# A two-layer hybrid encoder on one core: a static list scheduler gets other durations, a port rule and a table of priorities per layer

## The chip, the cores and the metric

The kernel runs on one core of a Trainium2 chip. The core has a matrix engine (PE, whose weight loads are listed apart as PEld), three engines for elementwise work (VectorE, listed as DVE; ScalarE, ACT; GpSimd, POOL) and SyncE (SP), whose queue issues nearly all transfers of this kernel. The metric is the device time of one execution, in microseconds (us).

## The reference

Two layers with `D_MODEL` 1024, 1024 tokens and a feed-forward width of 2816, all in float32. Each layer projects the residual stream once and gives the columns to four mixers: a Conformer convolution (31 taps), a bidirectional complex state-space layer (S5, 16 groups of 16 channels, 64 states each), a short gated convolution, and a differential attention with four heads. Cut to the loop over the layers:

```python
for l in range(DEPTH):
    h = jnp.einsum('bsd,de->bse', x, w_in[l])
    y_a = conformer_conv(h[..., :OFF_S5], ...)
    y_b = s5_mixer(h[..., OFF_S5:OFF_SC], ...)
    y_c = short_gated_conv(h[..., OFF_SC:OFF_DA], sc_conv_w[l])
    ...                       # q, k, v from h, partial rotary embedding of q and k
    y_d = diff_attention(q, k, v, lam, da_subln_g[l], lam_init)
    mix = jnp.einsum('bse,ed->bsd', jnp.concatenate([y_a, y_b, y_c, y_d], axis=-1), w_out[l])
    x = layer_norm(DEEPNORM_ALPHA * x + mix, ln1_g[l], ln1_b[l])
    ff = jax.nn.silu(x @ w_ffn1[l]) * (x @ w_ffn3[l])
    x = layer_norm(DEEPNORM_ALPHA * x + ff @ w_ffn2[l], ln2_g[l], ln2_b[l])
```

## The kernel before

**Arithmetic.** Matrix products keep float32 accuracy by splitting each operand into a high and a low part: a cast makes the high part, a subtraction the low one, and each product is three matmuls (`mm3`, L491; `split`, L497). So weights cost elementwise work: a cast and a `tensor_tensor` for each piece of 128x512. The products with the first and third feed-forward weights go by Winograd's form of Strassen's scheme: seven products in place of eight, and more additions on the weights (`make_unit`, L1335) and on the tokens (`token_operands`, L1283).

**Stages of a layer.** First the input blocks (`mixers_in`, L1430): per block of 256 columns either `chan_gemm` (psum tile `cg`) or `tok_gemm` (psum tile `tg`), and beside them the S5 layer in eight pairs of groups. A pair has tables (`s5_pair_tables`, L818; tiles `s5t`, made from the parameter tile `P`), then chunk sums, two scans and outputs (`s5_pair`, L876; work tiles `s5k`, psum tiles `s5wp`, `s5v`, `s5y`). The long convolution (`conf_conv`, L993) is a chain of multiply-adds into `acc` on DVE, then PE transposes (`cvt` there, `cvb` back) for its LayerNorm. Then come keys, values and queries (`kst`, `stg`, `vq` tiles), eight query tiles of attention (`sc` scores, `probs`, transposes `atp` to `aT`, `po` outputs), the output projection (`wo`) with the first LayerNorm (`xr`), and the feed-forward part (FFN): 11 chunks of hidden columns, each with an `up` product for w1, one for w3, and `dn` products with w2 into `r`. The split weight units of the FFN go through `wring`, a ring of four slots that `take` (L1358) fills from `upraw` and `w2raw`.

**What sets the order.** `Rec` (L49) records every call in program order as an operation of the class `Weaver`. `schedule` (L263) then simulates the five engines: an operation becomes ready when its inputs and its buffer slots are, each engine takes from its ready operations that with the lowest priority number, and each runs for the time that `cost` (L228) gives. The number is the index in program order plus `SHIFT` of the group; a group is the method that recorded the operation (the decorator `step`, L420). Operations recorded on `any2` may go to DVE or POOL, on `anyp` to ACT or DVE, on `any3` to all three; `schedule` takes the engine that would end first after adding the handicap `PREF` of the group and engine, in ns. `emit` (L412) issues the operations in the order found, so each engine's queue is fixed ahead of the run, and all instructions carry L417. Loads and stores of SP are ordered in the same way.

Of the kernel before, what the change touches and what calls it, by code (L numbers as in the profile page):

```python
# [18 lines left out]
P = 128  # L19
# [25 lines left out]
# rows of the per-channel parameter block  # L45
# [3 lines left out]
class Rec:  # L49
    """Records the calls on one engine for the Weaver."""  # L50
# [8 lines left out]
class Op:  # L59
    __slots__ = ("calls", "eng", "dur", "prio", "tail", "deps", "nout", "tiles", "succ", "left", "ready", "end", "start", "fset", "nb", "alt", "grp", "put")  # L60


class Weaver:
    """Static list scheduling: the kernel's instructions are recorded in program order, ordered per engine by
    data dependences, buffer slots and estimated durations, and issued to Tile in that order."""

    SHIFT = {"attn_finish": -13, "attn_heads": 6, "attn_q": 27345, "attn_v": 75687, "conf_a": 1270,
             "ffn_down": -170, "ffn_up": -163, "gain_rows": 153, "layer_norm": -11, "load_out": 17792,
             "load_raw": -1, "load_small": 597, "out_half": 5552, "q_stack": 2709, "s5_glu": -20,
             "s5_pair": -22755, "s5_pair_tables": -45599, "s5_params": -16108, "s5_u": 47110, "s5_ub": -3977,  # L70
             "short_b": -90, "short_c": 17, "short_v": 120, "to_xT": -1537, "token_operands": 3726}
    PREF = {"attn_finish gpsimd": -2764, "attn_finish scalar": -1516, "attn_finish vector": -1065,
             "attn_heads vector": 2866, "attn_k scalar": 2727, "attn_k vector": 1449,
             "conf_conv gpsimd": -1274, "conf_conv vector": 1485, "ffn_up gpsimd": -2667,
             "ffn_up scalar": -3000, "ffn_up vector": 835, "layer_norm gpsimd": -3000,
             "layer_norm scalar": -1677, "layer_norm vector": -2026, "load_in_block gpsimd": -1831,
             "load_in_block scalar": -213, "load_in_block vector": 112, "load_out gpsimd": -1596,
             "load_out scalar": -967, "load_out vector": 6000, "make_unit gpsimd": 491,
             "make_unit scalar": 1807, "make_unit vector": 2099, "q_stack scalar": -91,
             "s5_pair gpsimd": -46, "s5_pair vector": 257, "s5_pair_tables vector": 388,  # L80
             "token_operands gpsimd": 453, "token_operands vector": 1256}
    CHUNK = 1300.0
    WINDOW = 3413.0
    OUTS = ("out",)

    def __init__(self, nc, tc):
# [1538 lines left out]
```

## Time and profile before

| | |
|---|---|
| device time, median of 3 runs | 2556.78 us (2555.47 to 2559.75) |
| profiled execution, span | 2558.8 us, 32574 instructions |
| PE / PEld busy | 2354.7 us (92%) / 1950.2 us (76%) |
| DVE busy | 1831.7 us (72%) |
| POOL busy | 1464.4 us (57%) |
| ACT busy | 681.1 us (27%) |
| chain that ended last, by engine | PE 67%, DVE 21%, POOL 6% |

The page gives no other time of the profiled execution than its span; it lies 2.0 us above the median and within the three runs. The shares are averages over stages which differ, so the rows below give them by stage: mixers of the first layer to 300 us, keys and values to 365, attention to 578, FFN to 1237, the last products of the layer with the second LayerNorm to 1300, and the same again for the second layer.

### The profile page before, as it was taken

What the parts mean: (1) busy time and instruction counts of PE and PEld (TensorE: products, weight loads), DVE (VectorE), ACT (ScalarE), POOL (GpSimd) and SP (SyncE); (2) the same over time, 40 slices, a digit from 0 to 9 for tenths busy, and PEclk for the clock granted to TensorE, in tenths of its full rate; (3) what the DMA queues carried; (4) which work ended last, traced back from release to release, by engine and by line L of the source; (5) the groups of instructions that cost most, each with busy time, mean ns of one, the idle gap of its engine ahead of it and who ended that gap; (6) DMA issues with size and microseconds to landing.
All of it is one profiled execution on the core that took longest, in us unless ns stands there. A gap on an engine that the chain in (4) does not pass through costs nothing.

```text
span 2558.8 us, 32574 instructions
## 1 busy us (share of the span) xinstructions
PE 2354.7 (92%) x12412; PEld 1950.2 (76%) x12412; DVE 1831.7 (72%) x2611; ACT 681.1 (27%) x1172; POOL 1464.4 (57%) x1288
## 2 busy tenths in 40 slices
PE   8787898998999999999998779899989999999997
PEld 7666786776888888888786568777778888888886
DVE  6989868886565666656668998688866656666656
ACT  2211245553211121211212012555432112111120
POOL 1676753445655555555855776533465555555567
PEclk9888898998999999999999889899999999999998
DMA  4212111114111111111322112211231111111112
GB/s 134 71 37 62 59 57 63 63 60 148 58 50 56 52 50 50 58 51 57 108 75 70 25 55 77 68 52 61 79 132 54 54 55 53 58 58 50 50 50 99
DMA packets 126439, 167.59 MB, mean 65 GB/s; under 512 B 18432, under 2 KB 100940, under 8 KB 126028
## 3 DMA queue, kind: packets, MB, share of 16 engines
q1 hardware_dynamic: 126284, 165.52, 20.9%
q8 instruction: 98, 1.61, 0.3%
q14 instruction: 57, 0.47, 0.1%
HBM read 139.25 MB, written 26.25 MB: 65 GB/s over the span
## 4 chain that ended last, share of the span: by engine, by line
PE 67%; DVE 21%; POOL 6%; issue 2%; ACT 2%; DMA 2%; SPq 0%; POOLq 0%; DVEq 0%; ACTq 0%
PE up L417 33%; PE dn L417 16%; DVE acc L417 5%; PE tg L417 5%; PE wo L417 5%; DVE s5k L417 4%; DVE s5t L417 2%; DVE probs L417 1%; POOL r L417 1%; PE sc L417 1%; DVE asm L417 1%; PE cg L417 1%; POOL rs L417 1%; ACT probs L417 1%; DVE s5w L417 1%
## 5 line engine op out<-in xcount | busy, mean ns | idle before, releaser
L417 PE MATMUL up<-xT,wring 128*128 128x512 f32 x2112 | 486.2, 389 | 0.0
L417 PEld LDWEIGHTS up<-xT,wring 128*128 128x128 f32 x2112 | 396.4, 188 | 82.4 <-issue 0.2
L417 PE MATMUL dn<-wring,g 128*128 128x512 f32 x1920 | 452.0, 392 | 0.0
L417 PEld LDWEIGHTS dn<-wring,g 128*128 128x128 f32 x1920 | 360.7, 189 | 83.5 <-DVE r L417 7.4
L417 PE MATMUL up<-xB,wring 128*128 128x512 f32 x1584 | 371.0, 390 | 0.0
L417 PEld LDWEIGHTS up<-xB,wring 128*128 128x128 f32 x1584 | 297.7, 188 | 62.4 <-DVE xT L417 0.8
L417 DVE TENSOR_TENSOR r<-r,dn 128x512 f32<-128x512 f32 x288 | 197.4, 685 | 154.7 <-PE dn L417 151.9
L417 ACT CAST wring<-upraw 128x512 fp32r<-128x512 f32 x136 | 84.4, 622 | 547.5 <-PE dn L417 362.0
L417 PE MATMUL cg<-xh,win 128*128 128x512 f32 x640 | 221.6, 414 | 3.0 <-DVE sca L417 1.6
L417 PE MATMUL wo<-wout,yhl 128*128 128x512 f32 x768 | 201.7, 405 | 0.1
L417 PE MATMUL tg<-win,xh 128*128 128x256 f32 x1024 | 199.4, 293 | 1.6 <-ACT vq L417 1.6
L417 PEld LDWEIGHTS tg<-win,xh 128*128 128x128 f32 x1024 | 166.6, 198 | 4.9 <-ACT vq L417 1.9
L417 DVE TENSOR_REDUCE asm<-sc 128x1 f32<-128x1024 f32 x128 | 154.1, 1215 | 14.6 <-PE sc L417 14.1
L417 ACT ACTIVATE probs<-sc,asm 128x1024 f32<-128x1024 f32 x128 | 143.2, 1120 | 75.0 <-DVE asm L417 73.5
L417 PEld LDWEIGHTS wo<-wout,yhl 128*128 128x128 f32 x768 | 141.2, 192 | 27.9 <-POOL yhl L417 0.8
L417 PEld LDWEIGHTS cg<-xh,win 128*128 128x128 f32 x640 | 126.3, 197 | 37.1 <-issue 5.4
L417 PE MATMUL tg<-win,xl 128*128 128x256 f32 x512 | 149.6, 294 | 0.0
L417 POOL TENSOR_TENSOR wring<-upraw,wring 128x512 fp32r<-128x512 f32 x100 | 130.6, 1307 | 29.5 <-ACT wring L417 25.8
L417 DVE SCALAR_TENSOR_TENSOR acc<-conv,chp,acc 128x505 f32<-128x505 f32 (+8 forms) x154 | 146.6, 985 | 0.8
L417 DVE TENSOR_TENSOR tw<-tu,up 128x512 f32<-128x512 f32 x66 | 45.4, 687 | 139.0 <-PE up L417 139.0
L417 POOL TENSOR_TENSOR g<-sg,g 128x512 fp32r<-128x512 f32 x88 | 135.1, 1545 | 1.8 <-ACT g L417 1.8
L417 POOL TENSOR_TENSOR wring<-tw,wring 128x512 fp32r<-128x512 f32 x68 | 91.4, 1343 | 72.2 <-ACT wring L417 37.1
(243 smaller groups left out, 4198.7 us busy)
## 6 DMA issues: line engine op xcount, KB each, us to landing
upraw<-in_w_ffn_dram SPq DMA_DIRECT2D x88, 512.0 KB
w2raw<-in_w_ffn_dram SPq DMA_DIRECT2D x44, 512.0 KB
wraw<-in_w_in_dram SPq DMA_DIRECT2D x36, 512.0 KB
woraw<-in_w_out_dram SPq DMA_DIRECT2D x16, 512.0 KB
r<-x_scr SPq DMA_DIRECT2D x16, 512.0 KB
x_scr<-xr SPq DMA_DIRECT2D x14, 512.0 KB
yt<-yT_scr SPq DMA_DIRECT2D x16, 384.0 KB
x1row<-x_scr SPq DMA_DIRECT2D x12, 512.0 KB
```

The lines of the kernel that those rows point to most:

```text
L417: getattr(e, method)(*args, **kwargs)
```

## The change

Four things change. `cost` gets other durations. A new method `uses_port` marks operations of DVE and GpSimd, and `schedule` lengthens marked operations that overlap. The group of an operation gets the layer's number, so `SHIFT` and `PREF` have a row per layer. `CHUNK`, the length in ns up to which successive matmuls into one psum tile are planned as one operation (L196), goes from 1300 to 1370. The operations themselves, their data and the buffers stay as they are; comments are removed, which moves the line of `emit` from L417 to L461.

```diff
-    SHIFT = {"attn_finish": -13, "attn_heads": 6, "attn_q": 27345, "attn_v": 75687, "conf_a": 1270,
+    SHIFT = {"None": 3054, "attn_finish0": -4936, "attn_finish1": 564, "attn_heads0": -861, "attn_heads1": 1081,
...
-             "ffn_up scalar": -3000, "ffn_up vector": 835, "layer_norm gpsimd": -3000,
+            "attn_heads1 vector": 8000, "attn_k0 scalar": -2443, "attn_k0 vector": -593, "attn_k1 scalar": -1130,
...
-    CHUNK = 1300.0
+    CHUNK = 1370.0
     WINDOW = 3413.0
+    SHARE = 0.42
...
-                return max(27.0, (0.4167 if outs[0].dtype == F32R else 0.8334) * int(outs[0].shape[-1]) + 2.5), 0
+                n = int(outs[0].shape[-1])
+                return (max(85.0, 0.4167 * n + 13.3) if outs[0].dtype == F32R else max(62.0, 0.8334 * n + 2.5)), 0
...
-                return max(27.0, 0.4167 * n + 2.5), 0
+                return max(85.0, 0.4167 * n + 13.3), 0
             pair = int(outs[0].shape[0]) == 64
-            return max(108.0, 0.4167 * 4 * n) * (0.62 if pair else 1.0), 0
+            return max(108.0, 0.4167 * 4 * n + 5) * (0.57 if pair else 1.0), 0
...
+            if method == "tensor_tensor_scan":
+                return 68 + n / 0.52, 0
...
-            return 90 + 2.16 * n, 0
+            return 90 + 2.22 * n, 0
         if method == "tensor_copy":
-            return 90 + 3.36 * n, 0
+            return 90 + 0.95 * n, 0
         return 150 + 1.2 * n, 0
+
+    def uses_port(self, eng, method, outs, ins):
+        if eng == "gpsimd":
+            return method == "tensor_tensor"
+        if eng != "vector" or any(getattr(a.tensor, "_space", None) == PSUM for a in ins):
+            return False
+        if method in ("tensor_tensor", "scalar_tensor_tensor", "tensor_tensor_scan"):
+            return True
+        return method in ("tensor_scalar", "tensor_copy") and not any(getattr(a.tensor, "_space", None) == PSUM for a in outs)
...
             d = o.dur
+            port = o.alt[e][4] if o.alt else o.port
+            if port and e == "vector" and gp_end > s:
+                w = gp_end - s
+                d = d / self.SHARE if d <= w * self.SHARE else w + d - w * self.SHARE
+            elif port and e == "gpsimd" and dv_end > s:
+                w = min(dv_end - s, d)
+                d += 0.3 * w
+                free["vector"] += w * (1 / self.SHARE - 1) * 0.7
+            if port and e == "vector":
+                dv_end = s + d
+            elif port:
+                gp_end = s + d
...
-        old, w.group = w.group, f.__name__
+        old, w.group = w.group, f"{f.__name__}{self.layer}"
...
         for l in range(DEPTH):
+            self.layer = l
             self.mixers_in(l, xT, yT)
```

**The first S5 pairs on PE.** The first place is PE's queue in the first layer, where the first pair of S5 groups begins (`s5wp` and `s5k` are psum tiles of the pair's tables, `cg` a channel product of an input block, `win` its weights, `s5ut` transposed inputs, `s5v` chunk sums, `s5y` outputs). Before:

```order
L417 MATMUL s5wp_142<-ident,s5k_141 128x128 x4
L417 MATMUL s5k_143<-s5t_139 48x144 x4
L417 MATMUL cg_149<-xh_5_85,win_88 128x512
L417 MATMUL cg_149<-xl_7_87,win_88 128x512
L417 MATMUL cg_149<-xh_5_85,win_88 128x512 x2
L417 MATMUL cg_149<-xl_7_87,win_88 128x512
L417 MATMUL cg_149<-xh_5_85,win_88 128x512 x2
```

Now:

```order
L461 MATMUL s5ut_138<-ident,s5u_110 128x128 x4
L461 MATMUL s5wp_142<-ident,s5k_141 128x128 x4
L461 MATMUL s5k_143<-s5t_139 48x144 x4
L461 MATMUL s5wp_152<-ident,s5k_141 128x128 x4
L461 MATMUL s5k_153<-s5t_139 48x144 x4
L461 MATMUL s5v_154<-s5u_110,s5t_139 64x128 x8
L461 MATMUL s5wp_156<-ident,s5k_141 128x128 x4
L461 MATMUL s5k_157<-s5t_140,s5t_139 48x144 x4
L461 MATMUL s5y_155<-s5t_139,s5u_110 128x128
L461 MATMUL s5y_155<-s5t_139,s5k_141 128x128 x2
```

Before, products of the input blocks stand between the pairs: 144 `cg` matmuls of the first layer's 480 stand ahead of the first `s5wp`, and the other 336 follow it. Now all 480 stand ahead of it, with 96 `tg`, and the S5 instructions follow one another with no product between.

**Weights of the second layer's FFN on GpSimd.** The second place is GpSimd's queue in the second layer's FFN, in the same round of both (the weights `w2raw_1771` and `w2raw_1772` for the `dn` products, `upraw` for the next `up` products). Before:

```order
L417 TENSOR_TENSOR wring_1569<-upraw_1761,wring_1569 128x512
L417 CAST wring_1569<-upraw_1761 128x512
L417 TENSOR_TENSOR wring_1569<-upraw_1761,wring_1569 128x512
L417 TENSOR_TENSOR wring_1569<-w2raw_1771,wring_1569 128x512
L417 CAST wring_1569<-w2raw_1772 128x512
L417 TENSOR_TENSOR wring_1569<-w2raw_1771,wring_1569 128x512
L417 CAST wring_1569<-w2raw_1772 128x512
L417 TENSOR_TENSOR wring_1569<-w2raw_1772,wring_1569 128x512
L417 TENSOR_TENSOR tw_1591<-upraw_1777,upraw_1778 128x512
L417 TENSOR_TENSOR tw_1591<-tw_1591,upraw_1777 128x512
```

Now:

```order
L461 CAST wring_1569<-w2raw_1771 128x512
L461 TENSOR_TENSOR wring_1569<-w2raw_1771,wring_1569 128x512
L461 CAST wring_1569<-w2raw_1772 128x512
L461 TENSOR_TENSOR wring_1569<-w2raw_1772,wring_1569 128x512
L461 CAST wring_1569<-w2raw_1771 128x512
L461 TENSOR_TENSOR wring_1569<-w2raw_1771,wring_1569 128x512
L461 CAST wring_1569<-upraw_1777 128x512
L461 TENSOR_TENSOR wring_1569<-upraw_1777,wring_1569 128x512
L461 CAST wring_1569<-w2raw_1772 128x512
L461 TENSOR_TENSOR wring_1569<-w2raw_1772,wring_1569 128x512
L461 CAST wring_1569<-upraw_1778 128x512
```

In a round (one chunk of hidden columns) GpSimd's queue held 20 `tensor_tensor` and 7 casts, eight of the former the products of gate and value (`sg`, `g`). It now holds 26 `tensor_tensor` and 12 casts, all for weights; the `g` and `sg` products of this layer have gone to DVE.

**The convolution's end on PE.** The third place is PE's queue in the second layer where the first transposes of the convolution's result stand (`cvt`; `cvb` are those back, `tg` the products for keys, values and queries). Before:

```order
L417 MATMUL tg_1227<-win_1021,xh_938_1018 128x256 x2
L417 MATMUL cvt_1180<-ident,acc_1177 128x128
L417 MATMUL cvt_1180<-ident,acc_1178 128x128
L417 MATMUL cvt_1180<-ident,acc_1177 128x128
L417 MATMUL cvt_1180<-ident,acc_1178 128x128
L417 MATMUL cvt_1185<-ident,acc_1177 128x128
L417 MATMUL cvt_1185<-ident,acc_1178 128x128
L417 MATMUL cvt_1185<-ident,acc_1177 128x128
L417 MATMUL cvt_1185<-ident,acc_1178 128x128
L417 MATMUL tg_1227<-win_1021,xl_940_1020 128x256
L417 MATMUL tg_1227<-win_1021,xh_938_1018 128x256 x2
L417 MATMUL tg_1227<-win_1021,xl_940_1020 128x256
```

Now:

```order
L461 MATMUL tg_1237<-win_1022,xl_939_1019 128x256
L461 MATMUL cvt_1180<-ident,acc_1177 128x128
L461 MATMUL cvt_1180<-ident,acc_1178 128x128
L461 MATMUL cvt_1180<-ident,acc_1177 128x128
L461 MATMUL cvt_1180<-ident,acc_1178 128x128
L461 MATMUL cvt_1185<-ident,acc_1177 128x128
L461 MATMUL cvt_1185<-ident,acc_1178 128x128
L461 MATMUL cvt_1185<-ident,acc_1177 128x128
L461 MATMUL cvt_1185<-ident,acc_1178 128x128
L461 MATMUL cvb_1190<-ident,cxn_1179 128x128 x4
L461 MATMUL cvb_1191<-ident,cxn_1179 128x128 x4
L461 MATMUL cvt_1193<-ident,acc_1177 128x128
```

Before, `tg` products stood between the transposes, and some 285 of this layer's 768 `tg` matmuls behind the first `cvt`. Now the `cvt` and `cvb` stand in one row with no product between, and some 162 `tg` matmuls are left behind them. In the second layer the S5 pairs stand ahead of the `acc` chain on DVE, and PE's queue holds 54 `cg` and 450 `tg` between the last `s5y` and the first `sc`, where it held 402 `tg`.

**Instructions that change engine.** In the first layer's mixers DVE takes 77 `tensor_tensor` of the S5 part from GpSimd (`s5t<-P` 22 of 256 columns and 9 of 288, `s5t<-s5t` 10 and 7, `s5k<-s5k,s5t` 10, `s5k<-s5t,s5k` 8, 11 smaller), and GpSimd takes 13 casts of `win` from ACT and 3 from DVE. The second layer's mixers change likewise (some 70 instructions). In the first layer 16 casts of `kst` go from DVE to ACT, and in its attention 27 copies of `aT` from ACT to DVE, 9 casts of `stg` from DVE to ACT. In the second layer's attention DVE loses 3 casts of `stg`, 4 additions to `xr`, 4 casts of `yhl` and 2 of `wout`. In the first layer's FFN ACT takes most casts of weights (`wring<-upraw` 68 to 108, `w2raw` 21 to 40) and GpSimd nearly all their `tensor_tensor`, while DVE takes 23 `g` and 12 `sg` products. In the second DVE takes all 44 `g` and 44 `sg` products, the 44 casts of `g` and 22 copies of `tu` from ACT. At each layer's end the last load of `w2raw` stands behind the two loads of `ln` rows on SP's queue, where it stood ahead of them.

## Rows read from the trace of the kernel before

**Rows 1.** Busy time by stage: window, length, engines (instructions), granted clock, DMA share, GB/s.
```profile
core 0: us, PE busy (x) PEld busy (x) DVE busy (x) ACT busy (x) POOL busy (x), PEclk, DMA share, GB/s
0.00:300.00 300.00, 241.56 (x1358) 199.57 (x1358) 263.44 (x540) 59.96 (x100) 177.06 (x169) 0.91 0.25 70
300.00:365.00 65.00, 60.41 (x467) 59.10 (x468) 41.20 (x75) 21.22 (x33) 31.18 (x41) 0.89 0.20 65
365.00:578.00 213.00, 187.53 (x1347) 151.88 (x1345) 184.36 (x240) 120.16 (x219) 95.80 (x81) 0.96 0.19 63
...
624.00:1237.00 613.00, 613.00 (x2695) 504.58 (x2694) 367.02 (x452) 124.89 (x208) 353.12 (x294) 1.00 0.18 54
...
1300.00:1562.00 262.00, 214.38 (x1216) 177.98 (x1215) 225.26 (x326) 43.79 (x76) 173.07 (x161) 0.92 0.19 54
...
1627.00:1840.00 213.00, 186.97 (x1335) 151.37 (x1334) 184.13 (x240) 118.64 (x218) 94.52 (x77) 0.95 0.19 63
...
1884.00:2496.00 612.00, 612.00 (x2688) 503.67 (x2687) 367.62 (x451) 124.56 (x207) 352.83 (x294) 1.00 0.18 53
```

**Rows 2.** The chain that ended last, one FFN round: start, us, engine, tile, count.
```profile
698.37 38.08 PE up L417 x168
736.45 22.09 PE dn L417 x96
```

**Rows 3.** Waits of PE in 0:300: waiting tile, releaser, us, times, longest.
```profile
PE s5y L417 <- DVE s5k L417: 18.9, 8, 4.1
PE s5wp L417 <- POOL s5k L417: 14.7, 8, 3.5
```

**Rows 4.** Waits of PE in 1300:1562.
```profile
PE s5y L417 <- DVE s5k L417: 16.9, 7, 5.2
PE s5y L417 <- POOL s5k L417: 16.8, 4, 7.4
```

**Rows 5.** Timeline of the attention, DVE beside POOL: start, us, engine, operation.
```profile
484.18 1.28 DVE L417 SCALAR_TENSOR_TENSOR probs<-probs,asm 128x1024 f32<-128x1024 f32 x1
...
486.63 2.40 POOL L417 TENSOR_TENSOR xr<-xr,ln 128x1024 f32<-128x1024 f32 x1
...
486.78 3.33 DVE L417 SCALAR_TENSOR_TENSOR probs<-probs,asm 128x1024 f32<-128x1024 f32 x1
```

**Rows 6.** Timeline of the second layer's mixers, a cast on POOL beside DVE.
```profile
1385.84 2.33 POOL L417 CAST win<-wraw 128x1024 fp32r<-128x1024 f32 x1
...
1386.86 0.41 DVE L417 TENSOR_TENSOR s5t<-P 128x256 f32<-128x256 f32 x1
...
1388.71 0.73 DVE L417 SCALAR_TENSOR_TENSOR acc<-conv,chp,acc 128x504 f32<-128x504 f32 x1
```

**Rows 7.** Groups of DVE, shapes apart: count, busy us, mean ns, idle before.
```profile
L417 DVE TENSOR_TENSOR s5t<-P 128x256 f32<-128x256 f32 x47 | 30.9, 667 | 8.4 <-POOL s5t L417 8.1
...
L417 DVE TENSOR_TENSOR xr<-xr,ln 128x1024 f32<-128x1024 f32 x16 | 26.0, 1626 | 7.2 <-POOL xr L417 7.2
...
L417 DVE CAST kst<-ktp 128x512 fp32r<-128x512 f32 x32 | 21.0, 686 | 11.1 <-PE ktp L417 11.1
```

**Rows 8.** Groups of POOL, shapes apart.
```profile
L417 POOL TENSOR_TENSOR g<-sg,g 128x512 fp32r<-128x512 f32 x88 | 135.1, 1545 | 1.8 <-ACT g L417 1.8
L417 POOL TENSOR_TENSOR wring<-upraw,wring 128x512 fp32r<-128x512 f32 x100 | 130.6, 1307 | 29.5 <-ACT wring L417 25.8
...
L417 POOL CAST wring<-upraw 128x512 fp32r<-128x512 f32 x84 | 52.2, 622 | 91.4 <-DMA upraw<-in_w_ffn_dram 38.6 <-PE dn L417 29.9 <-PE up L417 20.5
L417 POOL TENSOR_TENSOR s5t<-P 128x256 f32<-128x256 f32 x49 | 43.4, 889 | 12.0 <-DVE s5t L417 6.1 <-DVE s5k L417 4.0
...
L417 POOL TENSOR_TENSOR sg<-sg,tu 128x512 f32<-128x512 f32 x22 | 38.3, 1739 | 0.0
...
```

**Rows 9.** The page's costliest groups, the convolution's chain on DVE.
```profile
L417 DVE SCALAR_TENSOR_TENSOR acc<-conv,chp,acc 128x505 f32<-128x505 f32 (+8 forms) x154 | 146.6, 985 | 0.8
```

**Rows 10.** The chain that ended last, 1536 to 1640.
```profile
1536.89 25.62 DVE acc L417 x28
...
1565.45 5.46 PE tg L417 x37
...
1571.79 2.64 PE tg L417 x22
...
1600.71 9.79 PE tg L417 x81
```

**Rows 11.** Waits of PE in the first layer's attention, 365:578.
```profile
PE sc L417 <- ACT probs L417: 12.1, 13, 3.5
```

**Rows 12.** SP's queue at the second layer's end: start, us, transfer.
```profile
2479.99 18.78 SPq L417 DMA_DIRECT2D w2raw<-in_w_ffn_dram  x4
2498.82 0.43 SPq L417 DMA_DIRECT2D ln<-in_ln_g_dram  x1
```

More of the change, by code (lines that the diff above doesn't have):

```diff
@@ L59 @@
 class Op:
-    __slots__ = ("calls", "eng", "dur", "prio", "tail", "deps", "nout", "tiles", "succ", "left", "ready", "end", "start", "fset", "nb", "alt", "grp", "put")
+    __slots__ = ("calls", "eng", "dur", "prio", "tail", "deps", "nout", "tiles", "succ", "left", "ready", "end", "start", "fset", "nb", "alt", "grp", "put", "port")
 class Weaver:
-    SHIFT = {"attn_finish": -13, "attn_heads": 6, "attn_q": 27345, "attn_v": 75687, "conf_a": 1270,
[L68 to L74, printed above, removed]
-             "ffn_up scalar": -3000, "ffn_up vector": 835, "layer_norm gpsimd": -3000,
[L76 to L81, printed above, removed]
-    CHUNK = 1300.0
+    SHIFT = {"None": 3054, "attn_finish0": -4936, "attn_finish1": 564, "attn_heads0": -861, "attn_heads1": 1081,
[11 rows of a table added]
+    PREF = {"attn_finish0 gpsimd": -6000, "attn_finish0 scalar": 7931, "attn_finish0 vector": -1759,
[18 rows of a table added]
+    CHUNK = 1370.0
     WINDOW = 3413.0
+    SHARE = 0.42
     OUTS = ("out",)
@@ L190, in record @@
                         m, a, k = "tensor_scalar", args, dict(op0=ALU.mult, op1=ALU.add)
-                alt[e] = self.cost(e, m, outs, ins, k, a)[0], m, a, k
+                alt[e] = self.cost(e, m, outs, ins, k, a)[0], m, a, k, self.uses_port(e, m, outs, ins)
             eng = min(alt, key=lambda e: alt[e][0])
@@ L203, in record @@
             op.fset, op.nb, op.alt = fset, 0, alt
+            op.port = alt[eng][4] if alt else self.uses_port(eng, method, outs, ins)
             op.tail = outs[0].tensor if eng == "tensor" else None
@@ L287, in schedule @@
         hot, busy, over, edge = False, 0.0, 0.0, self.WINDOW
+        gp_end = dv_end = 0.0
         def offer(o):
@@ L415, in emit @@
                 e = getattr(self.nc, o.eng)
-                for method, args, kwargs in [o.alt[o.eng][1:]] if o.alt else o.calls:
+                for method, args, kwargs in [o.alt[o.eng][1:4]] if o.alt else o.calls:
                     getattr(e, method)(*args, **kwargs)
@@ L432 @@
     COMB = ()
+    layer = 0
     def __init__(self, ctx, tc, t):
```

28 rows, old and new, of tables (PREF, SHIFT) are left out of this document.

## Prediction

> **What bounds the kernel now.** I read the busy time by stage first. The two FFN stretches show PE busy for all of 613 and 612 us at a granted clock of 1.00, the upper of its two levels [rows 1]; nothing in the order of the other engines can shorten them. In the chain that ended last a round there is 38.08 us of `up` and 22.09 us of `dn`, 60.17 us with no other engine between [rows 2]. So 1225 us of the span can only stay or grow, and they grow if a weight unit comes late.
>
> The rest is about 1334 us. In the mixers DVE is the fullest: 263.4 of 300 us in the first layer, 225.3 of 262 in the second, with PE at 241.6 and 214.4 and a mean clock of 0.91 and 0.92 [rows 1]. PE waits there for S5 tiles: in the first layer 18.9 us for DVE's and 14.7 for POOL's [rows 3], in the second 16.9 and 16.8 [rows 4]. In attention PE has 187 of 213 us and DVE 184 [rows 1], and the longest wait of PE is for ACT's exponentials, 12.1 us [rows 11].
>
> The third thing to see is how DVE and GpSimd slow each other. A `probs` update of DVE takes 1.28 us alone and 3.33 us where a GpSimd `tensor_tensor` of 2.40 us began 0.15 us before it [rows 5]: of the 2.25 us left it lost 2.05. Beside a GpSimd cast an `s5t` product took 0.41 us, though the same form means 0.67 over the run; an `acc` step took 0.73 us just after the cast [rows 6, 7], where the chain's mean is 0.985 [rows 9]. From these rows the surplus of the `acc` chain is 154 x (0.985 - 0.73) = 39 us and that of `s5t<-P` 47 x (0.667 - 0.41) = 12 us. Of GpSimd's operations the `tensor_tensor` costs DVE time; the cast does not, it pays itself.
>
> The Trainium skill (page "SBUF — State Buffer", section "Who interferes with whom") says that a DVE instruction with two inputs in SBUF contends with any GpSimd instruction that reads SBUF, and that the later starter is blocked for the whole of the other. The `probs` pair agrees with the blocking, nearly all of 2.25 us; the `s5t` product beside the cast does not agree with "any", and the measurement decides. The new planner halves the block (0.42 of the speed) and excludes casts; by the page's blocking its plan would be too mild, which makes the third rival below.
>
> **The change part by part.** The sum goes against the profiled span, 2558.8 us; that lies 2.0 us above the median and the runs spread over 4, so I take the difference off the median, 2556.8. For surplus per GpSimd time in the mixers I use an estimate made like the two above, over all DVE forms (each row's time beyond the shortest of its form): 80 us beside the 177 us of GpSimd in the first layer, 71 beside 173 in the second [rows 1], so 0.45 and 0.41 us of DVE for 1 us of GpSimd.
>
> 1. *First mixers.* DVE takes 77 S5 products at about 0.43 us alone (0.41 for the 256-column form [rows 6], up to 0.68), 33 us, and gives up 3 casts, about 4: 29 us more work. GpSimd loses 77 x 0.91 = 70 us (0.889 the commonest form [rows 8]), which by 0.45 gives DVE 31 back. The net is about -2 us. The waits of PE for POOL's `s5k`, 14.7 us, go with their cause, but DVE's are late next, since it now makes the tables itself. No channel product stands between the S5 pairs any more, so PE idles there where it was filled; against this PE gives the products earlier, and DVE's work is the same. I take -4. Bounds: -20 (all of POOL's wait goes, 14.7, and what the extra 16 casts on GpSimd free on ACT) to +15 (the returned 31 comes half only).
> 2. *First keys and values.* 16 `kst` copies at 0.686 us [rows 7] leave DVE: 11 us of its 41 in a stretch of 65, in which PE idles 4.6 [rows 1]. ACT has 21 of 65 and hides them. I take -3, bounds -4.6 and +2.
> 3. *First attention.* 27 copies of `aT` come to DVE. For a 128x512 read from psum its nearest row is 0.686 us [rows 7]: +18.5. Nine `stg` casts leave, -6.2, four of `yhl`, about -2: DVE has +10 on 184, and ACT, at 120, loses what DVE takes. DVE idles 29 us there, which covers part; ACT's exponentials come earlier, and 12.1 us of wait hang on them [rows 11]. I take +4, bounds 0 and +12 (nothing covered).
> 4. *First FFN.* ACT, with 125 of 613 us [rows 1], takes casts, GpSimd keeps products. No engine comes near the round's length: 0, bounds 0 and +3.
> 5. *Second FFN.* GpSimd makes nearly all weights: 26 `tensor_tensor` and 12 casts a round. At 1.307 and 0.622 us [rows 8] this is 34.0 + 7.5 = 41.5 of 60.2 us; before it had 352.8/612, or 34.7. The mean hides the deadline: the units due within the 38.1 us of `up` need 22 of the products and about 8 casts, 28.8 + 5.0 = 33.8 us. At the 1.545 us of `g<-sg,g`, a product of the same size and dearer, they need 39.0 (22 x 1.545 + 5.0). That is 0.9 us over, 9 for ten rounds; at 1.307 nothing. I take +2 and keep 0 and +9; the rows at 1.3 are for the very tiles, so I stand by them. DVE loses its weight products and gains the `g` and `sg` ones, whose only follower is the `dn` of the next round.
> 6. *Layer ends.* The last `w2raw` load moves behind two `ln` loads; a row of loads took 18.78 us for four [rows 12], and the two `ln` issues 0.43 each. The load has PE's last `dn` products waiting, but some 20 us after it was issued. I take +1, bounds -1 and +8.
> 7. *Second mixers.* As in 1, DVE +22 and GpSimd -64, which by 0.41 gives 27 back: -5. POOL's waits, 16.8 us [rows 4], go in part: -3. PE's work behind the convolution falls from 285 to 162 `tg` products at 9.79/81 = 0.12 us [rows 10], -14.6, since the chain `acc` then `cvt` then `tg` is the one that ends the stage. The transposes now stand without products between and expose their way over DVE and ACT, which I put at what the filling took before, 37 products in 5.46 us and 22 in 2.64 [rows 10], +8. Sum -14.6, taken as -14. Bounds -30 (the transposes stay hidden, POOL's wait goes whole) and +5 (the `acc` chain, now behind the S5 pairs, itself ends later by 20).
> 8. *Second attention.* DVE gives four `xr` additions at 1.626 us [rows 7] and nine smaller casts, -12 in all; GpSimd's four more `tensor_tensor` take back about 3. DVE idles 29 us here too, so two thirds count: -6, bounds -10 and +3.
>
> Sum: -4 - 3 + 4 + 0 + 2 + 1 - 14 - 6 = -20 us. 2556.8 - 20 = 2537 us.
>
> **Rivals.**
> *The second FFN turns GpSimd-paced: slower.* GpSimd would have `tensor_tensor` almost without a break beside DVE's new `g`, `sg` and cast work, all in SBUF. It decides from (38.1 - 5.0)/22 = 1.5 us a product on. For it: `g<-sg,g` 1.545 and `sg<-sg,tu` 1.739 us [rows 8], both under DVE. Against it: the weight groups at 1.3. At 1.64, between those two, a round has 41.0 of 38.1 us: +2.9, ten rounds +29 in place of +2, and 2564 us; at 1.739 it would be +51, and 2586.
> *The moved work is worth what it costs.* If DVE's freed time in the second mixers is used up by the transposes and the S5 pairs (term 7 at 0) and term 8 gives 0 since PE, with 187 of 213 us, has its own chain through ACT [rows 1, 11], the sum is -4 - 3 + 4 + 2 + 1 = 0: 2557 us. For it: PE's busy time does not change anywhere.
> *The later starter is blocked whole.* Then each GpSimd `tensor_tensor` taken out of the mixers is worth its full length to a DVE that is never idle: 70 + 64 = 134 us, less 29 + 22 us that DVE takes over, -83 in place of the -7 of terms 1 and 7: 2461; PE's own 55 us of idle time a stage allow about half, so 2495. For it: the `probs` pair [rows 5]. Against it: the 0.45 and 0.41 of the sum over all forms, for much of GpSimd's time falls on DVE work that reads psum. The page of the Trainium skill named above gives this rule.
>
> **How the numbers follow.** The forecast has 0.57, with an own range of 2515 to 2560, which takes in its terms' bounds where they don't all fall one way; the paced FFN 0.18; the even exchange 0.14; the full block 0.11. About 0.2%, 5 us, is what a measurement of this kernel can tell from no change. Faster are the full block and 0.52 of the forecast's 0.57, 0.63 together; within 0.2% the even exchange and 0.01 of the forecast, 0.15; slower the paced FFN and the forecast's last 0.04, 0.22. The range reaches from the full block's inner side to above the paced FFN's time: 2500 to 2570.
>
> **What would show it.** Right: the FFN stretch of the second layer still 612 us with PE at 100% and `wring` products of POOL at 1.3 us; the mixers of the second layer shorter by 10 to 15 us with the mean of `acc` nearer 0.73; `kst` copies on ACT. Wrong: `PE up` waiting for POOL's `wring` (second FFN); `acc` and S5 means on DVE as before (no return from GpSimd); a first attention over 217 us; a granted clock under 0.88 in the S5 stretch of the first layer, where PE stands unfilled; or a span under 2500, which would mean that the block is worth its full length.

## The result and the profile after

The changed kernel takes 2583.68 us (median of 4 runs, 2578.61 to 2584.89) against 2557.24 us for the kernel before in the same comparison: a ratio of 1.0097, 95% interval 1.0085 to 1.0110. It is slower by 1%, where 0.8% faster was forecast, and the time lies above the range of 2500 to 2570.

The profiled execution spans 2582.5 us. The page's first part, engine by engine (busy us, share of the span, instructions), shows where it did not come from:

```profile
PE 2354.8 (91%) x12412; PEld 1950.3 (76%) x12412; DVE 1762.0 (68%) x2689; ACT 657.9 (25%) x1123; POOL 1473.3 (57%) x1259
```

PE has the same work to 0.1 us, and DVE has 70 us less than before, POOL 9 us more. So the engines are not busier; they wait more. I cut both timelines at the same events (first score matmul `sc`, first and last `up`, first `tg` of the second layer) and took the lengths of the stretches:

| stretch, us | before | after | difference | forecast (terms) |
|---|---|---|---|---|
| first mixers, keys, queries, to the first `sc` | 352.8 | 375.4 | +22.6 | -7 (1, 2) |
| first attention, to the first `up` | 265.2 | 258.3 | -6.9 | +4 (3) |
| first FFN, first to last `up` | 618.8 | 615.6 | -3.2 | 0 (4) |
| layer end, to the first `tg` | 63.0 | 64.0 | +1.0 | } +1 (6) |
| second layer's end | 59.9 | 61.1 | +1.2 | } |
| second mixers, keys, queries | 312.5 | 300.1 | -12.4 | -14 (7) |
| second attention | 265.0 | 269.4 | +4.4 | -6 (8) |
| second FFN | 618.9 | 635.9 | +17.0 | +2 (5) |

Two stretches, +22.6 and +17.0, make the loss; the other six together give 16 us back.

**The second FFN.** The busy time by stretch (columns as in [rows 1]) shows PE no longer full:

```profile
634.00:1249.00 615.00, 615.00 (x2716) 509.04 (x2715) 306.99 (x390) 174.37 (x289) 390.56 (x285) 1.00 0.17 54
1886.00:2509.00 623.00, 611.95 (x2680) 501.63 (x2678) 370.82 (x458) 55.58 (x90) 460.35 (x396) 1.00 0.17 53
```

The first layer's FFN is still all PE; in the second 11 us are missing, with GpSimd at 460 of 623 us (352.8 of 612 before). The chain that ended last no longer reads 38.08 and 22.09 [rows 2]. In one round of it (start, us, engine, tile, count) PE's `dn` stands behind GpSimd and a transfer:

```profile
2090.00 5.46 PE up L461 x24
...
2098.20 3.56 DMA upraw<-in_w_ffn_dram
...
2105.58 1.74 POOL tw L461
...
2112.11 1.74 POOL upraw L461
2113.85 2.45 POOL wring L461 x2
...
2119.61 3.24 DMA w2raw<-in_w_ffn_dram
...
2123.67 1.28 POOL wring L461
...
2124.99 1.18 PE dn L461 x4
```

In this chain the raw weights of the next unit are loaded only when GpSimd has read the last ones, and the `dn` products start only when GpSimd has split what was loaded. From 2063.42 to 2124.99 a round takes 61.57 us, 1.4 more than the 60.17 before; PE's waits for it are listed as follows (waiting tile, releaser, us in total, times, longest), here for 1940:2440:

```profile
PE dn L461 <- POOL wring L461: 11.0, 17, 0.9
```

GpSimd's groups in the same stretch (count, busy us, mean ns, idle us before and what ended it), which answer to [rows 8]:

```profile
L461 POOL TENSOR_TENSOR wring<-upraw,wring 128x512 fp32r<-128x512 f32 x80 | 114.9, 1436 | 8.5 <-DVE wring L461 5.3
...
L461 POOL CAST wring<-upraw 128x512 fp32r<-128x512 f32 x56 | 39.5, 705 | 105.9 <-PE dn L461 62.4 <-DMA upraw<-in_w_ffn_dram 43.5
...
L461 POOL TENSOR_TENSOR tw<-upraw,upraw 128x512 f32<-128x512 f32 x16 | 24.2, 1512 | 0.0
```

The reader is to see two things. The products made from `upraw` and `tw` mean 1.42 to 1.52 us, where the first group meant 1.29 us in the same stretch before (1.307 over the run [rows 8]); those made from `w2raw` stay at 1.29. And GpSimd stands idle 106 us in these eight rounds, 13 a round, before its casts from `upraw`: it waits for PE to free a slot of `wring` and for the transfer. With the slot taken or the load on its way there is nothing to cast, so the full round was never GpSimd's to spend.

**The first mixers.** The order there was 480 channel products, then the S5 pairs, then token products. It isn't strict: 288 of the 768 token products stand ahead of the pairs, 96 more than before, and 59 among them. The rows by stretch, the S5 pairs in the middle:

```profile
83.00:196.00 113.00, 99.92 (x471) 83.72 (x470) 111.12 (x134) 5.96 (x11) 44.58 (x27) 0.94 0.21 63
196.00:314.00 118.00, 64.95 (x392) 52.53 (x393) 96.53 (x227) 17.64 (x39) 34.52 (x49) 0.68 0.13 27
314.00:375.00 61.00, 56.64 (x425) 50.91 (x424) 15.89 (x46) 28.55 (x49) 29.61 (x38) 0.97 0.19 60
```

PE idles 53 of 118 us in the middle at a mean clock of 0.68 between its two levels, and DVE idles 45 of 61 at the end. The same window of both kernels up to the first score, before and then after:

```profile
0.00:352.80 352.80, 289.78 (x1733) 247.05 (x1734) 293.38 (x603) 73.37 (x120) 199.85 (x199) 0.90 0.24 69
```

```profile
0.00:375.40 375.40, 293.04 (x1737) 250.31 (x1738) 284.31 (x661) 72.17 (x128) 132.50 (x137) 0.86 0.23 65
```

DVE has 9 us less work although it took 77 products over, PE 3 us more, and the stage is 23 us longer. The two engines overlap less: both are busy in 240 us before and in 217 after. The waits of PE up to the first score, against [rows 3]:

```profile
PE s5wp L461 <- DVE s5k L461: 23.0, 12, 3.3
PE s5y L461 <- DVE s5k L461: 16.4, 6, 8.6
PE s5y L461 <- POOL s5k L461: 8.0, 4, 5.2
```

and one more of the same window before:

```profile
PE s5wp L417 <- DVE s5k L417: 8.3, 3, 5.2
```

The waits for POOL's `s5k` at `s5wp`, 14.7 us, are gone; DVE's at the same tile went from 8.3 to 23.0.

**GpSimd's casts.** GpSimd has 14 casts of `win` in this window where it had one. One of them, the DVE product that began just behind it, and a product of the same form 8 us later (start, us, engine, operation):

```profile
69.71 1.04 POOL L461 CAST win<-wraw 128x1024 fp32r<-128x1024 f32 x1 [11.05 <-PE tg L461]
...
69.74 1.32 DVE L461 TENSOR_TENSOR s5t<-s5t 128x288 f32<-128x288 f32 x1
...
77.84 0.45 DVE L461 TENSOR_TENSOR s5t<-s5t 128x288 f32<-128x288 f32 x1
```

The product that began 0.03 us after the cast took 1.32 us for 0.45: it lost 0.87 of the 1.01 us that the cast had left.

### The profile page after: what moved, and what is told of

Same layout as the page of the kernel before. It is cut to its first block, busy times and chain, and to the rows that moved or that the text cites. A ratio compares the mean times of both kernels' runs of the same rounds, so it can differ in the third digit from the quotient of the medians.

```text
span 2582.5 us, 32510 instructions
## 1 busy us (share of the span) xinstructions
PE 2354.8 (91%) x12412; PEld 1950.3 (76%) x12412; DVE 1762.0 (68%) x2689; ACT 657.9 (25%) x1123; POOL 1473.3 (57%) x1259
## 5 line engine op out<-in xcount | busy, mean ns | idle before, releaser
L461 PE MATMUL up<-xT,wring 128*128 128x512 f32 x2112 | 486.1, 389 | 0.0
L461 PE MATMUL dn<-wring,g 128*128 128x512 f32 x1920 | 453.1, 392 | 16.1 <-POOL wring L461 15.8
L461 PEld LDWEIGHTS up<-xT,wring 128*128 128x128 f32 x2112 | 396.3, 188 | 82.5 <-DVE xT L461 0.3
L461 PEld LDWEIGHTS dn<-wring,g 128*128 128x128 f32 x1920 | 360.2, 188 | 99.1 <-POOL wring L461 24.1
L461 PE MATMUL up<-xB,wring 128*128 128x512 f32 x1584 | 370.3, 389 | 0.2 <-DVE xT L461 0.2
L461 PEld LDWEIGHTS up<-xB,wring 128*128 128x128 f32 x1584 | 297.0, 188 | 62.2 <-DVE xT L461 0.6
L461 DVE TENSOR_TENSOR r<-r,dn 128x512 f32<-128x512 f32 x288 | 197.5, 686 | 198.7 <-PE dn L461 198.7
L461 POOL TENSOR_TENSOR wring<-upraw,wring 128x512 fp32r<-128x512 f32 x210 | 289.8, 1384 | 52.8 <-ACT wring L461 39.5
L461 PE MATMUL cg<-xh,win 128*128 128x512 f32 x640 | 209.5, 401 | 8.2 <-DVE conv L461 5.3
L461 PE MATMUL tg<-win,xh 128*128 128x256 f32 x1024 | 200.0, 294 | 8.7 <-DVE sca L461 6.9
L461 PE MATMUL wo<-wout,yhl 128*128 128x512 f32 x768 | 198.1, 402 | 0.4 <-DVE xr L461 0.4
L461 PEld LDWEIGHTS tg<-win,xh 128*128 128x128 f32 x1024 | 167.5, 199 | 12.6 <-issue 8.7
L461 DVE TENSOR_REDUCE asm<-sc 128x1 f32<-128x1024 f32 x128 | 154.9, 1216 | 32.2 <-PE sc L461 31.7
L461 POOL TENSOR_TENSOR wring<-tw,wring 128x512 fp32r<-128x512 f32 x88 | 128.4, 1459 | 69.2 <-ACT wring L461 63.0
L461 PEld LDWEIGHTS wo<-wout,yhl 128*128 128x128 f32 x768 | 142.0, 191 | 29.9 <-POOL yhl L461 1.0
L461 ACT ACTIVATE probs<-sc,asm 128x1024 f32<-128x1024 f32 x128 | 143.1, 1120 | 80.9 <-DVE asm L461 80.5
L461 PEld LDWEIGHTS cg<-xh,win 128*128 128x128 f32 x640 | 122.4, 191 | 37.6 <-DVE conv L461 6.2
L461 PE MATMUL tg<-win,xl 128*128 128x256 f32 x512 | 149.1, 293 | 0.0
L461 ACT CAST wring<-tw 128x512 fp32r<-128x512 f32 x64 | 39.7, 620 | 390.1 <-POOL tw L461 283.9
L461 DVE SCALAR_TENSOR_TENSOR acc<-conv,chp,acc 128x507 f32<-128x507 f32 (+8 forms) x154 | 133.2, 891 | 1.9
L461 POOL TENSOR_TENSOR wring<-w2raw,wring 128x512 fp32r<-128x512 f32 x80 | 104.3, 1304 | 49.7 <-ACT wring L461 46.4
L461 ACT ACTIVATE sg<-sg 128x512 f32<-128x512 f32 x88 | 55.6, 632 | 280.0 <-DVE sg L461 280.0
```

The source lines that it names most:

```text
L461: getattr(e, method)(*args, **kwargs)
```

## The experiments

Each run is read by its stretches (same cuts as above), since several totals hide two changes of opposite sign. The kernel before ran on the same chip each time, at 2556.8 to 2559.1 us.

**e1, the order alone.** The S5 rows of the first layer's mixers, and their other `SHIFT` rows, go back (those of keys, values and queries stay).

```diff
-"s5_pair0": -1746, "s5_pair_tables0": -986, "s5_u0": 5464, "conf_a0": -6158,
+"s5_pair0": -22755, "s5_pair_tables0": -45599, "s5_u0": 47110, "conf_a0": 1270,
...
```

> The changed kernel with the order numbers (SHIFT) of the first layer's mixers as before the change: 360 of the 480 channel products stand between the S5 pairs again, while 201 of the 214 S5 products that the change gave to DVE in this layer stay on DVE. Theory 'unfilled': the first layer's mixers lost 23 us because PE has no products between the S5 pairs (PE 65 of 118 us busy there, granted clock 0.68); filled again, the mean clock of the stretch is 0.83 or more, the first score matmul comes 15 to 25 us earlier (about 355 us, changed kernel 375), and the time is 2559 to 2569 us. Rival 'engines': DVE is late because it took the S5 products over; then the first score stays within 5 us of 375 and the time within 5 of 2584.

Measured: 2582.89 us (ratio 1.0088, 1.0073 to 1.0103). The first score came at 365.3 us, 10 earlier; the second FFN took 644.0 us in place of 635.9 and kept 8 of it. Neither theory holds. The pairs are filled and end at 267 in place of 314, but PE then stands at the convolution's transposes (waits of PE in 235:370):

```profile
PE cvt L432 <- DVE acc L432: 29.4, 2, 27.8
```

Behind the waiting `cvt` PE's queue holds 288 token products which need nothing of it. My 'unfilled' was half of the story: DVE has two chains in this stage, the pairs and the convolution, and what counts, as I read it, is when both are done. In this run the convolution's last step ended at 319 us, against 235 in the changed kernel.

**e2, order and engines.** As e1, with the `PREF` rows of the stage as before.

```diff
-"s5_pair_tables0 gpsimd": 7478, "s5_pair_tables0 vector": -706, "load_in_block0 gpsimd": -3582,
+"s5_pair_tables0 vector": 388, "load_in_block0 gpsimd": -1831,
...
```

> The changed kernel with both tables (SHIFT and PREF) of the first layer's mixers as before: 360 channel products between the S5 pairs, and 116 S5 products on GpSimd again where the change left 34. Theory 'unfilled': as the run with the order alone, within 5 us of it (2559 to 2569). Rival 'engines': about 2560 here and no gain with the order alone, so the two runs lie 15 us or more apart.

Measured: 2586.32 us (1.0108), first score 370.0: with the S5 products on GpSimd again it is 5 us worse than with them on DVE. 'Engines' falls as well. There must be a cause that both edits leave in place.

**e3, the second FFN like the first.**

```diff
-"make_unit1 gpsimd": 294, "make_unit1 scalar": 1378, "make_unit1 vector": 5181, "ffn_up1 scalar": 3168,
+"make_unit1 gpsimd": 533, "make_unit1 scalar": -3322, "make_unit1 vector": 2156, "ffn_up1 scalar": -2470,
...
```

> The changed kernel with the FFN rows of the second layer set to those of the first layer: 11 of 12 casts a round go from GpSimd to ACT, half of the gate products from DVE to GpSimd; the products for weights stay on GpSimd. Theory 'GpSimd paces the second FFN': PE's waits for GpSimd's wring units (1.6 us a round, 17 us in all) vanish, the stretch from first to last up product goes from 635.9 to about 616 us, the time to 2564 to 2569. Rival 'something else is late in the second FFN (the load of w2raw by its own)': the waits stay, 2580 or more.

Measured: 2561.66 us (1.0003, 0.9993 to 1.0013), a little under the range. The stretch took 616.2 us, and PE was busy in all of 1940:2440, here first in the changed kernel and then in this run:

```profile
1940.00:2440.00 500.00, 489.81 (x2140) 401.08 (x2141) 299.25 (x373) 39.35 (x64) 356.21 (x306) 1.00 0.17 52
```

```profile
1940.00:2440.00 500.00, 500.00 (x2207) 414.01 (x2206) 247.94 (x320) 132.47 (x221) 304.59 (x224) 1.00 0.18 53
```

So the second layer's own FFN rows cost 19.7 us. Over the whole stretch 13.2 of them were idle time of PE before `dn` (622.7 of 635.9 us busy); the rest goes with longer records of `dn`, 206.3 us in all against 197.5 here.

**e4, e1's stage with both tables and e3 together.**

> Both edits together: first layer's mixers with both tables of before, second layer's FFN with the first layer's rows. If the two causes are apart and add up: 2584 - 20 - 18 = about 2546 us, which is faster than the kernel before (2557) by 0.4%. If one gain is given back by the other stage (attention or the second mixers starting in another state), 2555 to 2565.

Measured: 2563.33 us (1.0016, 1.0007 to 1.0026), the first score at 368.3, second FFN 616.4, but the second mixers at 310.7 in place of 300.1. The sum failed in the first stage, which gave 7 us and not 20, and a stage that nobody touched lost 10. With the same rows GpSimd is busy there for 150.5 us in place of 138.0, so its plan is another one; the likely reason is that it begins from another state.

**e5, the fourth corner of order by engine.** The changed order, S5 products on GpSimd.

```diff
-"s5_pair0": -1746, "s5_pair_tables0": -986, "s5_pair_tables0 gpsimd": 7478, "s5_pair_tables0 vector": -706,
+"s5_pair0": 754, "s5_pair_tables0": 1514, "s5_pair_tables0 gpsimd": 0, "s5_pair_tables0 vector": 388,
```

> The changed kernel with the S5 products of the first layer on GpSimd as before the change (113 there and 135 on DVE; changed kernel 34 and 214), but in the changed order: all 480 channel products ahead of the first S5 pair, none between the pairs. With the run of the order alone (first score matmul 365.3 us) and the changed kernel (375.4) this fills the third corner of the table order by engine. Theory 'two chains on DVE': the stage ends when DVE has done the S5 pairs and the convolution and PE the products that are left, so neither edit alone returns to 353: here 365 to 385. Rival 'engines': DVE gets 33 us of work less, the first score comes at 353 to 360.

Measured: 2602.15 us (one run), first score 390.0, outside both. PE waits 47.7 us for GpSimd's `s5k`:

```profile
PE s5wp L432 <- POOL s5k L432: 29.4, 10, 4.9
PE s5y L432 <- POOL s5k L432: 18.3, 6, 4.9
```

So giving the products to DVE is worth 15 us in the new order and 5 in the old: it was right. What loses is the order, or the rule that was on in all four.

**e6, the first stage planned as before.** Durations, `CHUNK`, table and the missing port rule of the kernel before for the groups of that stage alone, and e3's edit.

```diff
+    OLD = {'s5_pair0', 's5_pair_tables0', 'conf_conv0', 'attn_k0', ...}
     def cost(self, eng, method, outs, ins, kw, args):
+        if self.group in self.OLD:
+            return self.cost_old(eng, method, outs, ins, kw, args)
...
     def uses_port(self, eng, method, outs, ins):
+        if self.group in self.OLD:
+            return False
```

> The changed kernel in which the operations of the first layer's mixers, keys, values and queries are planned by the durations, the table and without the port rule of the kernel before (its order there is the one before: 144 channel products ahead of the first S5 pair, 336 between), and the second layer's FFN has the first layer's rows. Theory 'the new plan of that stage is the loss': the first score at 353 us (changed kernel 375), the rest as in the run with the FFN rows alone, so 2561 - 22 = 2540 us, 0.7% faster than before. Rival 'the loss comes back elsewhere' (attention gives 7 us less, as it began later): 2545 to 2556.

Measured: 2550.11 us (0.9964, 0.9951 to 0.9976), faster than before. The first score is at 353.9. The rival holds for the rest: attention took 261.8 us (258.3 in the changed kernel) and the second mixers 308.2 (300.1).

**e7, the old table under the new durations.** `SHIFT` and `PREF` of before for both layers.

> The new durations, the port rule and the new CHUNK with the table of before in both layers. Theory 'table': the loss is in the numbers fitted per layer; with the old ones the second FFN stays at 616 to 619 us from first to last up and the total at 2550 to 2565. Theory 'durations': the old numbers were fitted to the old durations, so under the new ones the order is again another (most weight casts go to GpSimd, since the new duration of a cast there is a third), and the first mixers lose 10 to 20 us in waits of the transposes for the convolution: 2565 to 2590.

Measured: 2631.61 us (1.0286, 1.0264 to 1.0308); the first score at 370.2, the FFNs at 637.6 and 632.9 us (read from an execution of 2640.86 us, the longest of the four). 'Table' falls: the old numbers are bad under the new durations, worse than the new numbers are, and the total lies beyond the range of 'durations' too.

**e8, only the casts off GpSimd.** The `make_unit1` rows of `PREF` in e3 alone.

> The changed kernel in which only the handicaps of the second layer's weight units are those of the first layer: the 130 casts of weights leave GpSimd for ACT and 15 weight products go to DVE, while DVE keeps all gate products, casts of g and copies of tu, so that the port is shared as much as in the changed kernel. Theory 'load': GpSimd sheds 7 to 8 us a round and PE's waits for wring vanish: last up minus first up 616 to 619 us (changed 635.9), time 2562 to 2570. Theory 'port': GpSimd's products at 1.5 to 1.74 us beside DVE's are late all the same: 625 to 636 us.

Measured: 2569.18 us (one run), second FFN 621.5. GpSimd's products stayed as dear or dearer:

```profile
L432 POOL TENSOR_TENSOR wring<-tw,wring 128x512 fp32r<-128x512 f32 x32 | 49.0, 1532 | 13.6 <-ACT wring L432 13.6
...
L432 POOL TENSOR_TENSOR upraw<-upraw 128x512 f32<-128x512 f32 x16 | 27.9, 1742 | 0.0
```

and PE's waits for `wring` in 1940:2440 fell from 11.0 to 0.4 us. That is 14.4 of the 19.7 us by GpSimd's load alone, nearly all of it casts; the time lies between the two ranges that I had set, and what the 5 us that are left hang on is open.

**e9, the first stage without the port rule.** Table of before (keys, values and queries too), new durations, e3's FFN.

```diff
     def uses_port(self, eng, method, outs, ins):
+        if self.group in self.OLD:
+            return False
```

> First layer's mixers, keys, values and queries by the table of before and the new durations, with the port rule left out for the operations of that stage alone; second layer's FFN with the first layer's rows. The order then has 436 token products behind the first transpose of the convolution, as the kernel before has 399, while with the port rule the same table leaves 288. Theory 'port rule': the rule makes the plan of that stage, not the durations; the first score comes at 350 to 358 us (368 to 370 with the rule) and the total is 2540 to 2552. Rival 'durations': the first score stays at 365 to 372, the total at 2555 to 2565.

Measured: 2546.69 us (0.9954, 0.9937 to 0.9970), the fastest of all, 0.46% faster than the kernel before. First score 357.9, the upper end of what 'port rule' gave.

**e10, the port rule alone on the old plan.** The stage by durations and table of before, the rule on.

> The same with the opposite choice: that stage by the table and the durations of before, and the port rule put on top (288 token products behind the first transpose). Theory 'port rule': first score at 365 to 372 us, total 2553 to 2565. Rival 'durations': 350 to 358, total 2540 to 2552.

Measured: 2557.93 us (1.0000, 0.9990 to 1.0009), first score 366.2. In that stage e6 differs from it by the rule alone, with the first score at 353.9: the rule costs 12.3 us of the stage and 7.8 of the total. Under the new durations e7 and e9 are such a pair, 370.2 and 357.9, 12.3 again. (From e9 to e10 the durations change as well, so their 8.3 us is not the rule's price.) The long wait is there in e10 and gone in e9 (waits of PE to the first score, then those from 280 on); in e6 it is 3.3:

```profile
PE cvt L435 <- DVE acc L435: 16.2, 2, 14.7
```

```profile
PE cvt L437 <- DVE acc L437: 4.9, 2, 2.5
```

**e11, the new table under the old durations**, with neither rule nor new CHUNK.

> The new table per layer with the durations of before and no port rule anywhere. If the table was fitted to the new durations and is worth something only with them: first score later than 375 us, second FFN above 636 us since nearly no cast stays on GpSimd but all gate products go to DVE (so this may also go down to 620), total 2580 to 2620. If the port rule is what harms, the first mixers come back to 355 to 365 us.

Measured: 2589.58 us (one run); first score 376.0, second FFN 627.4. The first theory's total holds, and of its second FFN the lower way out. The first mixers don't come back without the rule, so under the old durations the table's rows have a loss of their own: 23.2 us against the kernel before, which differs in that stage by the table alone.

**e12, casts of g and copies of tu to ACT.**

```diff
-"ffn_up1 scalar": 3168
+"ffn_up1 scalar": -2470
```

> The changed kernel in which the 44 casts of g and the 22 copies of tu of the second layer's FFN go from DVE back to ACT; GpSimd's queue there is the same (26 products and 12 casts a round). Theory 'load': last up minus first up stays at 632 to 640 us (changed kernel 635.9). Theory 'port': DVE is in SBUF 4 to 6 us less a round, GpSimd's products of the up phases go from 1.51 towards 1.3 us, and the stretch falls to 620 to 628.

Measured: 2578.32 us (one run), second FFN 636.3, with GpSimd's `tw` products still at 1.52 us (`upraw<-upraw` fell from 1.52 to 1.35). 'Load' holds; taking DVE's casts away didn't shorten the stretch.

**e13, the new table without the rule in the first stage.**

> The changed kernel with the port rule left out for the first layer's mixers, keys, values and queries, its own table there (480 channel products ahead of the first S5 pair all the same), and the second FFN with the first layer's rows. With table old or new and rule on or off there are then four corners; three are known (first score: old, off 354 to 358; old, on 366 to 370; new, on 375). Theory 'rule alone': taking it out brings this corner to 355 to 362 us too. Theory 'the table by itself as well': its order (S5 pairs late and unfilled) is the loss here, 370 to 380 us, and the time 2555 to 2566.

Measured: 2576.93 us (one run), first score 382.5, beyond what 'the table by itself as well' gave (370 to 380), as is the total, and far from 'rule alone'. The corners of that stage, first score in us (four runs with the changed kernel's rows there, e3, e8, e12 and itself, read 373.7 to 375.4, so a difference under 2 us says nothing):

| | rule off | rule on |
|---|---|---|
| table of before, old durations | 352.8 (before), 353.9 (e6) | 366.2 (e10) |
| table of before, new durations | 357.9 (e9) | 370.2 (e7); with the new rows for keys, values and queries 368.3 (e4), 370.0 (e2) |
| new table, old durations | 376.0 (e11) | |
| new table, new durations | 382.5 (e13) | 375.4 (changed kernel) |

On the old table the rule costs 12 us under either durations. Without the rule the new table costs 23 (old durations) to 25 (new); with the rule it is 7 better than without, and still 22.6 us later than the kernel before. The new durations with the new `CHUNK` cost 4 (e6 to e9).

**e14, the rule out of both mixer stages.**

> As the run without the rule in the first layer's stage (2547 us; old table there), and the rule left out in the second layer's mixers, keys, values and queries too, whose table stays the new one. Theory 'the rule harms wherever DVE ends the stage': second mixers 293 to 300 us (303 with it) and 2537 to 2544. Theory 'the second layer's table was fitted with the rule in place and needs it': 305 to 320 us and 2549 to 2564.

Measured: 2551.64 us (0.9979, 0.9969 to 0.9988); the second mixers took 304.0 us, 302.9 with the rule. The total falls into the second theory's range and the stretch misses it by 1 us; a difference of 1 us in the stretch says that the rule neither made nor spoilt the gain of the second mixers.

## Why the prediction was wrong

*Term 1, the first mixers, is the first step that failed.* "The net is about -2 us ... I take -4", with +15 as the worst, and 23 us were lost together with term 2. The count of work had the right sign: to the first score DVE's 293.4 us fell to 284.3, 9 where terms 1 and 2 have 13 (2, and 11 of `kst` casts). The fault is the sentence that DVE's work is the same and PE gives its products earlier. Work by engine says nothing of a stage in which two engines must overlap. Before, both of DVE's chains ended late and together (pairs at 283, convolution at 302 us in the timeline) with products beside both. After, the convolution's steps stood first (the last at 235), the channel products beside them, and the pairs came last and alone, to 313. The sign that I had named, an unfilled stretch with a clock under 0.88, was there at 0.68; it had no price in the sum and no chance among the rivals, for the +15 stood for another cause, GpSimd's time coming back by half.

The runs showed that filling it isn't enough while the rule is on (e1, e2, e4), that the engine choice was good (e5), and that two planning edits each lose here by themselves: the port rule 12.3 us (e6 to e10) and the rows of the new table 23 to 25 (the kernel before to e11, e9 to e13). They don't add: with the new rows in place the rule gives 7 us back, so the rows alone are enough for the loss of the changed kernel. In all runs with the old order the first score came 46 to 52 us after the later of DVE's two chains had ended, in all with the new order 62 to 67. How the rule does it is argued and not shown: it makes DVE's operations longer in the plan, and the order that comes out ends the pairs at 265 and the convolution at 319 us (e10), where e6 has 284 and 303.

*Term 5, the second FFN, is the second.* The rival was right that GpSimd paces that FFN, and in the sign; the waits are at `dn`, not at `up` where I had looked for them. I held +2 as likeliest and gave the rival +29; it is +17.0, and 19.7 against the first layer's rows (e3). The rival's own price didn't come about: it decides from 1.5 us a product on, those made from `upraw` and `tw` mean 1.46 together, and by its sum (22 x 1.46 + 5.0 = 37.1 of 38.1 us) PE would not have waited. The failed step is "at 1.307 nothing", by which GpSimd had 38.1 us for 33.8 us of work. The 38.1 us aren't free: 13 us a round go by before a slot and a load let GpSimd begin. A deadline has to be counted from the moment the buffer comes free. That the casts' load weighs more than dear products is shown by e8, where the products are as dear and 14.4 of the 19.7 us come back, and by e12, where DVE does less beside GpSimd and nothing comes back.

*Terms 3 and 8, the attentions*, +4 and -6, came out at -6.9 and +4.4, both outside their bounds, the sum nearly as forecast. In the first the waits of PE for ACT's `probs` fell from 12.1 [rows 11] to 6.0 us though DVE took 27 copies; DVE's busy time fell from 225.9 to 220.6 us. In the second the waits of the transposes for DVE's `probs` grew from 5.2 to 12.0. No run tells which edit did it.

*Terms 7, 4 and 6* came near: -12.4 for -14, -3.2 for 0 (just outside its bounds of 0 and +3), +2.2 for +1. In term 7 the way was another. PE's waits at S5 tiles fell from 43 to 16 us in the stretch (the POOL ones of [rows 4] from 16.8 to 4.8). The transposes took 16 back, where I had 8: `cvt` waits for `acc` longer (before, then after), and `cvb` another 4.9 us for DVE's `cxn`.

```profile
PE cvt L417 <- DVE acc L417: 4.6, 2, 3.0
```

```profile
PE cvt L461 <- DVE acc L461: 16.0, 2, 10.6
```

The sign that I had named, `acc` steps nearer 0.73 us, isn't there: they mean 0.953 in this stage and meant 0.949. That the number came so near is in part luck: with the same rows in this stage it took 300.0 us in e8 and 310.7 in e4.

*The even exchange* failed with the result. *The full block* too. To the first score DVE took some 29 us of work over and gave 11 away, and is 9 us less busy, so 27 came back while GpSimd's busy time fell by 67 (199.85 to 132.50): 0.40 of it, where I had 0.45 and the rival needed 1. The Trainium skill (page "SBUF — State Buffer", section "Who interferes with whom") states the block for instructions that share the port, and the pair of [rows 5] agrees. That the rest of GpSimd's time over a stage meets no such instruction is argued, not shown.

*"The cast does not"* was misread. The prediction took from [rows 6] that a GpSimd cast costs DVE nothing. In that row the cast took 2.33 us, against 1.04 for the one shown above: it was the cast that lost time there, and DVE that went ahead. In the rows at 69.71 it is the other way round: the cast took its 1.04 us and the product lost 0.87. What decides which of the two waits isn't shown. By an estimate over such pairs, each product's time beyond the shortest of its form, the 14 casts took DVE some 8 us of the first stage. So the "any" that the prediction set aside by its row stands in this trace, and the port rule of the new planner, which leaves casts out, misses them.

## What to carry to other kernels

When a scheduler moves whole chains, don't add up busy time: lay the ends of the chains beside each other, and ask what runs beside the last one. Count a feeder's deadline from the time its buffer comes free, with the durations it has under load, not over the round. And a model change and a table fitted to it must be judged stage by stage: a total can hold -10 in one stage and +8 in another (e1), and the best version here leaves the rule and the new rows out of the first stage and uses the first layer's FFN rows in both (e9, 2546.69 us).

## What the hardware showed unasked

In the second FFN of the changed kernel GpSimd's `tensor_tensor` of 128x512 took 1.27 to 1.32 us with no DVE instruction beside it, or with one that has an input in psum (`r<-r,dn`), and 1.60 to 1.75 beside DVE's `sg` products and casts of `g`, whose inputs all lie in SBUF. DVE's cast of that size meant 1.40 us there (`g<-sg`, 32 in 44.8 us), against 0.73 for its casts from `upraw` and 0.69 for a copy from psum (`tu<-up`). Taking the 44 casts of `g` and 22 copies of `tu` off DVE left GpSimd's `tw` products at 1.52 us (e12).
